# A Conformer without modulation blocks, part of its sums and copies on VectorE, ones products issued later, and a convolution lag of two

## The chip, the cores and the metric

The kernel runs on one core of a Trainium2 chip. The time is the device time of one execution in microseconds (us). A core has five engines that run side by side, each through its own queue in the order in which instructions were put there: TensorE (PE, matmuls; its weight loads are PEld), VectorE (DVE), ScalarE (ACT), GpSimd (POOL) and SyncE (SP, which here issues nearly all DMAs). They wait for each other through semaphores.

## The reference

A decoder trunk on one sequence of 1024 positions with 1024 channels. Layer 0 is an mLSTM block and layer 1 a Conformer convolution; after each comes a gated feed-forward block with a short convolution (ConvFFN). Each of the four blocks is preceded by a norm whose shift and scale, and followed by a gate, that come from a conditioning vector `c`: a product of `c` with a matrix gives 6 x 1024 numbers per layer. The block around which most of the change lies:

```python
def conformer_conv_block(h, w_pw1, b_pw1, dw_w, dw_b, ln_g, ln_b, w_pw2, b_pw2):
    a, gte = jnp.split(h @ w_pw1 + b_pw1, 2, axis=-1)
    u = a * jax.nn.sigmoid(gte)
    u = causal_dwconv(u, dw_w, dw_b)          # 31 taps
    u = jax.nn.silu(layernorm(u, ln_g, ln_b)) # over the 1024 channels
    return u @ w_pw2 + b_pw2
```

## The kernel before

**Layout.** Channels lie on the 128 partitions, in 8 blocks; the sequence lies along the free axis, in two halves `h` of 512 columns. Every float32 operand of a large product is split into two fp32r parts (`split`: ScalarE casts the high part, line 191, VectorE subtracts it, line 192), and each product of 128x128 by 128x512 becomes three matmuls (`proj_k`, line 220; `chain_products`, line 507, in products that use a scheme with seven instead of eight products). Weights come as 512 KB loads `raw` through SyncE's queue and are split into `wu`.

**What sets the order.** The program is emitted in Python order, generators interleave parts by hand (`yield` and `steps`), and a tile scheduler with priorities then gives each engine's order; tiles come from pools with a fixed number of buffers, and a tile's next user waits for the last reader.

**Modulation blocks.** `ada_product` (line 153) makes 128 channels of the modulation: a 512 KB load (line 155) and one VectorE product of 128x1024 with an accumulated sum (line 156, with a read of the accumulator); `ada_bias` (162) adds the bias and `scale_of` (186) turns scales and norm gains into `sclA`. `adas(n)` takes the next n of the list `blocks_left`: 32 of layer 0 and 48 of layer 1, in this order. They are spread over: the mLSTM's up-projection, one for each i from 3 on (13), and its z stage, 7 or 6 for each j (40); the up-projection of layer 0's ConvFFN, one in each j from 4 on until 16 (`LATER`) are left (11, there in tiles called `rb`); and the second pointwise product of the Conformer, two for each of 8 m (16, in tiles `ada`, with `c` loaded once more as `crep1`).

**The Conformer.** First the pointwise product for blocks 0 to 3 and both halves, whose 31-tap convolution runs on VectorE (`conv_dve`, 30 steps of line 1725 per block, woven in by `filler`). Blocks j = 4 to 7 (`TAIL`) follow for each half: two products (`proj`), `glu` and `spread`, and a convolution on TensorE, `conv_pe`: `spread` lays the channels out anew in `u4` (through DRAM, lines 1681 and 1683; for j = 7 by 16 ScalarE copies, line 1673), 36 matmuls with banded weights follow (line 1703; the profile shows two for each), whose bands `bands(j)` loads through POOL's queue into 4 buffers, and 16 evacuations on ScalarE add the bias (line 1712). `conv_pe(j, h)` waits in the list `ready` and runs after the two products of the next j.

**LayerNorm.** `layer_norm(h)` sums the 8 channel blocks by 8 products with a matrix of ones (line 1621, two matmuls each in the profile), centres them (1623, VectorE), squares them (1628, ScalarE), sums these by 8 more (1629), takes the inverse root (1632, 1633), and makes the operands `s8` of the next product (1637, 1638, `split`). `first` (h = 0) is stepped along the second half's loop. `second` (h = 1) begins after the last convolution and is stepped behind the second pointwise products m = 3 to 7 of h = 0; three of these products (`lead`) were started before. Each product is followed by `residual` (502, VectorE), and `following`, which squares and sums for the next norm (271, 272); L281 is that norm's product with ones. The bias of the residual is added at line 1792.

Of the kernel before, what the change touches and what calls it, by code (L numbers as in the profile page):

```python
# [15 lines left out]
P = 128  # L16
# [63 lines left out]
def trunk(ctx, tc, a):  # L80
# [20 lines left out]
    def ps(shape=(P, HS)):  # L101
        return psum.tile(list(shape), F32, tag="ps", name=nm("ps"), padded_shape=[P, HS])
# [590 lines left out]
    LATER = 16  # L693
# [17 lines left out]
    def ffn_up(layer, normed, p_d, hx, ux, es_u, other, ops):  # L711
# [149 lines left out]
        for j in range(LEAD, FB):  # L861
            s = Seven(pairs.pop(j), right, HALF)
            s.ready = set()
            if j < FB - 1:
                if layer == 0 and j > LEAD and len(blocks_left[1]) > LATER:
                    adas(1)
                    if len(blocks_left[1]) == LATER:
                        scale_of(1, 0, 0, KB)
# [129 lines left out]
    def mlstm(normed, x0, keep, k1, es1, es_x0, xp, con):  # L998
# [6 lines left out]
        if True:  # L1005
# [64 lines left out]
            with ExitStack() as es_z:  # L1070
# [65 lines left out]
                for i, h, o in stream:  # L1136
# [3 lines left out]
                    if h == NHALF - 1:  # L1140
# [10 lines left out]
                        if i >= 3:  # L1151
                            adas(1)
# [182 lines left out]
                for j in range(2, KB):  # L1335
                    s = seven[j] = Seven(pairs[j], right, HALF)
                    s.ready = set()
                    for n, q in enumerate(ORDER):
                        step(j, q)
                        adas(n < 7 - (j > 5))  # L1340
# [256 lines left out]
    def conformer(normed, following):  # L1597
# [18 lines left out]
        def layer_norm(h):  # L1616
# [3 lines left out]
            for j in range(KB):  # L1620
                pe.matmul(om, ones, at[j], start=j == 0, stop=j == KB - 1)
# [3 lines left out]
            ov = ps()  # L1625
            for j in range(KB):
                t = t512()
                sc.activation(t, at[j], AF.Square)
                pe.matmul(ov, ones, t, start=j == 0, stop=j == KB - 1)
# [31 lines left out]
        def spread(j, h, o, sg):  # L1661
# [6 lines left out]
            if j == KB - 1:  # L1668
                v.scalar_tensor_tensor(sg, o, pv("bpw1", j), sg, ALU.add, ALU.mult)
                s4 = sg.rearrange("p (n r) -> p r n", r=4)  # L1670
                for g in range(4):
                    for r in range(4):
                        sc.copy(u4[32 * r : 32 * r + 32, g, :], s4[32 * g : 32 * g + 32, r, :])
# [23 lines left out]
        def conv_pe(j, h):  # L1697
            for g in range(4):
# [12 lines left out]
                for q in range(4):  # L1711
                    sc.activation(  # L1712
                        y4[32 * g : 32 * g + 32, 3 - q, n0 : n0 + N4],
                        o[32 * q : 32 * q + 32],
                        AF.Identity,
                        bias=dwb4[32 * q : 32 * q + 32, 4 * j + g : 4 * j + g + 1],
                    )
# [33 lines left out]
        for h in range(NHALF):  # L1751
            for j in range(TAIL, KB):
# [6 lines left out]
                while ready:  # L1759
                    ready.pop(0)()  # L1760
                bands(j)
# [20 lines left out]
        ca = es_y.enter_context(phase("ca", side="right"))  # L1782
        crep = ca.tile([P, D], F32, name="crep1")
        dma(crep, crep_d)
        ada_[:] = crep, ada_tiles(ca, 2)
# [7 lines left out]
        for h in range(NHALF):  # L1793
            for m in range(KB):
# [4 lines left out]
                if not h:  # L1799
                    if m >= lead:  # L1800
                        steps(second, (1, 1, 2, 3, 3)[m - lead])
                    adas(2)
                    if m == KB - 1:
                        scale_of(1, 1, 0, KB)
# [142 lines left out]
```

## Time and profile before

| what | value |
|---|---|
| time, median of 3 runs | 2617.64 us (2614.78 to 2620.78) |
| the profiled execution | 2619.32 us, span 2617.5 us |
| mean granted TensorE clock | 0.985 |
| busy: PE, DVE, ACT, POOL | 96%, 84%, 51%, 7% |
| DMA, mean over the span | 150 GB/s |

The lines of the profile name an engine, the line of the kernel, what is written and what is read, the shape and the count. Busy times are microseconds, means are nanoseconds. Behind a bar, or in brackets, stands how long the engine was idle just before, and what it then waited for. "Clock" is the share of TensorE's full rate that was granted. The Conformer's gates (L1687) run from 1558 to 1788 us and its second pointwise product ends at 1934 us; the up-projection of layer 0's ConvFFN begins at about 890 us.

### The profile page before, as it was taken

The page shows a single profiled execution, that of the slowest core. Times are in us where ns is not written, and L with a number is a line of the kernel's source. Part 1 is how long each engine was busy: PE and PEld are TensorE (multiplying, and loading weights), DVE is VectorE, ACT ScalarE, POOL GpSimd, SP SyncE. Part 2 cuts the span into 40 slices and gives each one's busy share as a digit, 9 for nine tenths or more (in the row PEclk, how much of TensorE's full clock was granted, in tenths as well). Part 3 has the DMA queues.
Part 4 walks back from the last instruction along what each step waited for, and adds up shares of the span by engine and source line. Part 5 has one row for each costly group of instructions (what it writes and reads, how often), then busy time and mean ns, then how long its engine had stood idle before and what let it go on. Part 6 is the DMA issues. An engine that isn't in the chain of part 4 may idle for free.

```text
span 2617.5 us, 31554 instructions
## 1 busy us (share of the span) xinstructions
PE 2501.1 (96%) x11421; PEld 2044.4 (78%) x11421; DVE 2203.5 (84%) x3064; ACT 1329.6 (51%) x2005; POOL 177.4 (7%) x320
## 2 busy tenths in 40 slices
PE   6999899999999999999999999999798999999998
PEld 4788688788778778888877888877576888887787
DVE  8988986787867899998889679992889998888866
ACT  6544445776634554444544342458564444444434
POOL 0232201332100000000000000000000000000000
PEclk9999899999999999999999999999999999999999
DMA  8676355432676234433354331545823332336422
GB/s 306 191 216 206 120 201 185 132 114 70 217 271 215 93 133 161 153 117 101 116 199 148 121 140 50 171 148 165 264 85 117 121 117 101 109 97 219 151 81 97
DMA packets 149085, 393.85 MB, mean 150 GB/s; under 512 B 14848, under 2 KB 36544, under 8 KB 148928
## 3 DMA queue, kind: packets, MB, share of 16 engines
q1 hardware_dynamic: 144320, 372.95, 43.0%
q0 software_dynamic: 4608, 18.88, 2.2%
q8 instruction: 90, 1.47, 0.2%
q14 instruction: 67, 0.55, 0.1%
HBM read 299.46 MB, written 92.31 MB: 150 GB/s over the span
## 4 chain that ended last, share of the span: by engine, by line
PE 67%; DVE 18%; DMA 6%; ACT 6%; issue 3%; SPq 0%; DVEq 0%; ACTq 0%
PE ps L507 41%; PE ps L220 19%; DVE cy L1725 5%; DVE h L192 3%; PE ps L1448 2%; PE ps L1485 2%; DVE wu L192 2%; DMA ada<-in_ada 1%; ACT cy L1712 1%; DMA raw<-xc_d 1%; ACT h L191 1%; PE ps L1102 1%; DMA raw<-p_d 1%; DVE ada L156 1%; ACT wu L191 1%
## 5 line engine op out<-in xcount | busy, mean ns | idle before, releaser
L507 PE MATMUL ps<-h,wu 128*128 128x512 f32 x4704 | 1098.5, 392 | 20.5 <-DVE wu L192 6.8
L507 PEld LDWEIGHTS ps<-h,wu 128*128 128x128 f32 x4704 | 884.1, 189 | 219.9 <-DVE wu L192 10.2
L220 PE MATMUL ps<-h,wu 128*128 128x512 f32 (+1 forms) x2574 | 608.3, 392 | 13.2 <-ACT h L191 6.2
L220 PEld LDWEIGHTS ps<-h,wu 128*128 128x128 f32 x2574 | 480.3, 190 | 122.6 <-ACT h L191 7.8
L191 ACT CAST wu<-raw 128x1024 fp32r<-128x1024 f32 (+1 forms) x286 | 298.4, 1045 | 299.6 <-PE ps L220 89.5
L192 DVE TENSOR_TENSOR wu<-raw,wu 128x1024 fp32r<-128x1024 f32 (+1 forms) x286 | 346.8, 1213 | 69.6 <-ACT wu L191 68.8
L840 DVE SCALAR_TENSOR_TENSOR c<-u,par,c 128x1024 f32<-128x1024 f32 x176 | 219.9, 1279 | 2.5 <-ACT c L838 2.4
L838 ACT ACTIVATE c<-u,par 128x1024 f32<-128x1024 f32 x88 | 108.5, 1243 | 107.5 <-DVE u L627 98.2
L507 PE MATMUL ps<-h,w 128*128 128x512 f32 x648 | 157.3, 390 | 1.9 <-DVE w L192 1.9
L1725 DVE SCALAR_TENSOR_TENSOR cy<-cu,par,cy 128x512 f32<-128x512 f32 (+1 forms) x180 | 156.0, 926 | 1.1 <-ACT cy L1721 0.3
L507 PEld LDWEIGHTS ps<-h,w 128*128 128x128 f32 x648 | 121.5, 188 | 28.0 <-DVE w L192 2.8
L502 DVE SCALAR_TENSOR_TENSOR x<-ps,mod,x 128x512 f32<-128x512 f32 (+1 forms) x140 | 97.9, 715 | 43.3 <-PE ps L220 35.5
L192 DVE TENSOR_TENSOR h<-raw,h 128x512 fp32r<-128x512 f32 (+1 forms) x160 | 105.1, 688 | 25.1 <-ACT h L191 24.9
L191 ACT CAST h<-raw 128x512 fp32r<-128x512 f32 (+1 forms) x160 | 91.4, 605 | 64.7 <-DMA raw<-p_d 28.1
L1448 PE MATMUL ps<-q,h 128*128 128x512 f32 (+2 forms) x576 | 115.3, 349 | 0.3 <-DVE q L192 0.3
L1448 PEld LDWEIGHTS ps<-q,h 128*128 128x128 f32 x576 | 94.9, 189 | 16.0 <-ACT t L1513 2.0
L156 DVE SCALAR_TENSOR_TENSOR ada<-ada,crep 128x1024 f32<-128x1024 f32 x69 | 83.0, 1215 | 22.4 <-DMA ada<-in_ada 22.1
L750 ACT ACTIVATE c<-c 128x1024 f32<-128x1024 f32 x44 | 46.7, 1061 | 94.6 <-DVE c L840 94.5
L728 POOL MEMSET u<- 128x2 f32 x88 | 8.4, 99 | 1123.4 <-DVE c L840 686.6
L220 PE MATMUL ps<-h,h 128*128 128x512 f32 (+1 forms) x450 | 83.6, 347 | 0.0
L220 PEld LDWEIGHTS ps<-h,h 128*128 128x128 f32 x450 | 72.4, 189 | 10.5
L1703 PEld LDWEIGHTS ps<-u,wband 128*128 128x128 f32 x576 | 66.9, 195 | 4.1 <-issue 3.7
(282 smaller groups left out, 3240.0 us busy)
## 6 DMA issues: line engine op xcount, KB each, us to landing
raw<-in_fup SPq DMA_DIRECT2D x94, 512.0 KB, 3.6
ada<-in_ada SPq DMA_DIRECT2D x85, 512.0 KB, 4.6
p_d<-c SPq DMA_DIRECT2D x44, 512.0 KB, 2.7
raw<-in_pw SPq DMA_DIRECT2D x40, 512.0 KB, 3.8
wband<-in_w POOLq DMA_DIRECT2D x32, 576.0 KB, 5.5
raw<-in_mup SPq DMA_DIRECT2D x32, 512.0 KB, 4.4
raw<-in_fdownS SPq DMA_DIRECT2D x32, 512.0 KB, 4.2
raw<-in_mdown SPq DMA_DIRECT2D x24, 512.0 KB, 4.4
```

What stands on the lines that cost most here:

```text
L156: v.scalar_tensor_tensor(w, w, 1.0, crep, ALU.mult, ALU.mult, accum_out=mod[:, layer, b : b + 1])
L191: sc.copy(out_hi, raw)
L192: (engine or v).tensor_tensor(out_lo, raw, out_hi.bitcast(F32), ALU.subtract)
L220: pe.matmul(o, t[:, i, c : c + P], acts[k][:, j, :], start=k == 0 and n == 0, stop=k == nk - 1 and n == 2,)
L502: v.scalar_tensor_tensor(xs, o, gate, xs, ALU.mult, ALU.add)
L507: pe.matmul(o, w[:, i, k * P : (k + 1) * P], acts[k][:, j, :], start=first and k == 0 and q == 0, stop=last and k == n - 1 and q == 2, ski ...
L838: sc.activation(c, body(b), AF.Identity, scale=taps[FK - 1], bias=pv("fcb", layer, b))
L840: v.scalar_tensor_tensor(c, u[b][:, i : i + S], taps[i], c, ALU.mult, ALU.add)
L1448: pe.matmul(so[:, tlo:], xr[cc][I // nJ][:, i, I % nJ * P : (I % nJ + 1) * P], un["qs"][cc][:, j, tlo:], start=n == 0, stop=n == 3 * CB - 1,)
L1485: pe.matmul(un["num"][cc][:, tlo:], vr[I][:, i, cc * P : (cc + 1) * P], pt[:, j, tlo:], start=I == 0 and n == 0, stop=I == nJ * (hf + 1) - ...
L1703: pe.matmul(o, wd[:, 4 * d : 4 * d + 4, :].rearrange("p d c -> p (d c)"), phases[j][:, g, n0 + d : n0 + d + N4], start=d == 0, stop=d == 8,)
L1725: v.scalar_tensor_tensor(y, u[:, t + c0 : t + c1], pv("dww", t, j), y, ALU.mult, ALU.add)
```

## The change

Four things change.

1. Modulation blocks: none in the Conformer any more. The mLSTM's up-projection takes one from i = 1 on (15) and its z stage 7 for every j (42); layer 0's ConvFFN takes one for each j from 3 on, and two from j = 16 on (23). Both `scale_of` of layer 1 stand there, at the end.
2. `layer_norm(1)` adds its 8 channel blocks on VectorE (7 additions) and takes one product with ones, for the mean and for the squares; the products are issued a `yield` later, and `steps` behind m = 3 to 7 are 2, 0, 2, 4, 4 instead of 1, 1, 2, 3, 3.
3. For h = 1, half of the convolution's evacuations (odd g) and half of the copies of j = 7 (even g) go to VectorE.
4. In h = 0 a convolution runs after the products of the j after the next. The first half thus leaves two in `ready`; both run at j = 4 of the second half, with the loads of the bands of j = 7 between them.

```diff
-                if layer == 0 and j > LEAD and len(blocks_left[1]) > LATER:
-                    adas(1)
-                    if len(blocks_left[1]) == LATER:
-                        scale_of(1, 0, 0, KB)
+                adas(1 + (j >= 2 * CHUNK))
+                if layer == 0 and not blocks_left[1]:
+                    scale_of(1, 0, 0, KB)
+                    scale_of(1, 1, 0, KB)
...
-                        if i >= 3:
+                        if i:
                             adas(1)
...
-                        adas(n < 7 - (j > 5))
+                        adas(1)
...
             om = ps()
-            for j in range(KB):
-                pe.matmul(om, ones, at[j], start=j == 0, stop=j == KB - 1)
+            if h:
+                total = t512()
+                v.tensor_tensor(total, at[0], at[1], ALU.add)
+                for j in range(2, KB):
+                    v.tensor_tensor(total, total, at[j], ALU.add)
+                yield
+                pe.matmul(om, ones, total, start=True, stop=True)
+            else:
+                for j in range(KB):
+                    pe.matmul(om, ones, at[j], start=j == 0, stop=j == KB - 1)
...
             ov = ps()
+            total = t512()
             for j in range(KB):
-                t = t512()
+                t = t512() if j or not h else total
                 sc.activation(t, at[j], AF.Square)
-                pe.matmul(ov, ones, t, start=j == 0, stop=j == KB - 1)
+                if not h:
+                    pe.matmul(ov, ones, t, start=j == 0, stop=j == KB - 1)
+                elif j:
+                    v.tensor_tensor(total, total, t, ALU.add)
+            if h:
+                yield
+                pe.matmul(ov, ones, total, start=True, stop=True)
             yield
...
-                        sc.copy(u4[32 * r : 32 * r + 32, g, :], s4[32 * g : 32 * g + 32, r, :])
+                        (sc.copy if g % 2 or not h else v.tensor_copy)(
+                            u4[32 * r : 32 * r + 32, g, :], s4[32 * g : 32 * g + 32, r, :]
+                        )
...
+                    if h and g % 2:
+                        v.tensor_scalar(y, o[32 * q : 32 * q + 32], bias, None, ALU.add)
+                    else:
+                        sc.activation(y, o[32 * q : 32 * q + 32], AF.Identity, bias=bias)
...
-                while ready:
+                while len(ready) > 1 - h:
                     ready.pop(0)()
-                bands(j)
+                    if h and j == TAIL and ready:
+                        bands(KB - 1)
+                if h or j > TAIL:
+                    bands(j - 1 + h)
...
-        ca = es_y.enter_context(phase("ca", side="right"))
-        crep = ca.tile([P, D], F32, name="crep1")
-        dma(crep, crep_d)
-        ada_[:] = crep, ada_tiles(ca, 2)
...
-                if not h:
-                    if m >= lead:
-                        steps(second, (1, 1, 2, 3, 3)[m - lead])
-                    adas(2)
-                    if m == KB - 1:
-                        scale_of(1, 1, 0, KB)
+                if not h and m >= lead:
+                    steps(second, (2, 0, 2, 4, 4)[m - lead])
```

In the new kernel some lines carry other numbers: the convolution's matmuls are L1719, its evacuations L1731 (VectorE) and L1733 (ScalarE), the taps on VectorE L1741, the ones products of h = 1 L1625 and L1643, centring L1630, the squares' additions L1640, the reciprocal L1647.

TensorE before, where the first convolution (j = 4, h = 0) stands; the row above and the rows below it are products of pointwise blocks (each row three matmuls into `ps_1928`, `ps_1943`):

```order
L220 MATMUL ps_1928_13177<-h_1836_12332,wu_1924_13137 128x512 x3
L220 MATMUL ps_1928_13177<-h_1838_12337,wu_1924_13137 128x512 x3
L1703 MATMUL ps_1929_13202<-u4_1920_13119,wband_1915_13109 128x128 x9
L1703 MATMUL ps_1930_13216<-u4_1920_13119,wband_1916_13111 128x128 x9
L1703 MATMUL ps_1931_13230<-u4_1920_13119,wband_1917_13113 128x128 x9
L1703 MATMUL ps_1932_13244<-u4_1920_13119,wband_1918_13115 128x128 x9
L220 MATMUL ps_1943_13289<-h_1818_12233,wu_1927_13174 128x512 x3
```

TensorE now, where the third and the fourth convolution (j = 6 and 7, h = 0) stand at the start of the second half:

```order
L220 MATMUL ps_1988_13615<-h_1888_12622,wu_1984_13582 128x512 x3
L1719 MATMUL ps_1989_13640<-u4_1964_13412,wband_1977_13550 128x128 x9
L1719 MATMUL ps_1990_13654<-u4_1964_13412,wband_1978_13552 128x128 x9
L1719 MATMUL ps_1991_13668<-u4_1964_13412,wband_1979_13554 128x128 x9
L1719 MATMUL ps_1992_13682<-u4_1964_13412,wband_1980_13556 128x128 x9
L1719 MATMUL ps_1997_13704<-u4_1982_13560,wband_1993_13696 128x128 x9
L1719 MATMUL ps_1998_13718<-u4_1982_13560,wband_1994_13698 128x128 x9
L1719 MATMUL ps_1999_13732<-u4_1982_13560,wband_1995_13700 128x128 x9
L1719 MATMUL ps_2000_13746<-u4_1982_13560,wband_1996_13702 128x128 x9
L220 MATMUL ps_2010_13783<-h_1872_12540,wu_1987_13612 128x512 x3
```

Every convolution of the first half has moved behind one more pair of pointwise products, and the last two stand together.

VectorE before, in the second LayerNorm, from its centring on (`csc1` is the inverse root, `ada` a modulation block's tile, `x` the residual stream):

```order
L1623 SCALAR_TENSOR_TENSOR cy7_12591<-ps_2081_14443,cy7_12591 128x512
L502 SCALAR_TENSOR_TENSOR x_2079_14428<-ps_2071_14268,mod_77,x_2079_14428 128x512
...
L156 SCALAR_TENSOR_TENSOR ada_2083_14470,mod_77<-ada_2083_14470,crep1_14433 128x1024
L192 TENSOR_TENSOR wu_2111_14603<-raw_2110_14601,wu_2111_14603 128x1024
L156 SCALAR_TENSOR_TENSOR ada_2084_14473,mod_77<-ada_2084_14473,crep1_14433 128x1024
L162 TENSOR_TENSOR mod_77<-mod_77,par_72 128x2
L1633 RECIPROCAL csc1_12594<-csc1_12594 128x512
L156 SCALAR_TENSOR_TENSOR ada_2085_14478,mod_77<-ada_2085_14478,crep1_14433 128x1024
L156 SCALAR_TENSOR_TENSOR ada_2086_14481,mod_77<-ada_2086_14481,crep1_14433 128x1024
```

VectorE now, from the last convolution's evacuations to the reciprocal (`t512_2099` is the sum of the channels, `t512_2107` that of the squares):

```order
L1731 TENSOR_SCALAR cy7_12651<-ps_2094_14471,dwb4_12659 32x128 x4
L1623 TENSOR_TENSOR t512_2099_14500<-t512_2099_14500,cy7_12651 128x512
L502 SCALAR_TENSOR_TENSOR x_2096_14489<-ps_2088_14329,mod_77,x_2096_14489 128x512
L1630 SCALAR_TENSOR_TENSOR cy0_12644<-ps_2098_14499,cy0_12644 128x512
...
L1640 TENSOR_TENSOR t512_2107_14566<-t512_2107_14566,t512_2108_14568 128x512
L192 TENSOR_TENSOR wu_2119_14622<-raw_2118_14620,wu_2119_14622 128x1024
L1640 TENSOR_TENSOR t512_2107_14566<-t512_2107_14566,t512_2109_14571 128x512
L502 SCALAR_TENSOR_TENSOR x_2096_14489<-ps_2117_14594,mod_77,x_2096_14489 128x512
...
L1640 TENSOR_TENSOR t512_2107_14566<-t512_2107_14566,t512_2114_14586 128x512
L1647 RECIPROCAL csc1_12654<-csc1_12654 128x512
```

The blocks' rows are gone, the additions have come, and the reciprocal stands behind the last addition of squares. On TensorE the mean's single product stands behind the products of m = 3, the squares' behind those of m = 4 and 5.

VectorE now, late in layer 0's ConvFFN up-projection, where before no block stands (`rb` is a block's tile):

```order
L156 SCALAR_TENSOR_TENSOR rb_1494_10046,mod_77<-rb_1494_10046,ra_1227_7843 128x1024
L162 TENSOR_TENSOR mod_77<-mod_77,par_72 128x2
L753 TENSOR_TENSOR c_1423_9469<-c_1423_9469,c_1422_9452 128x1024
L192 TENSOR_TENSOR wu_1434_9549<-raw_1433_9547,wu_1434_9549 128x1024
L653 TENSOR_TENSOR t512_1424_9476<-c_1423_9469 128x512
L558 TENSOR_TENSOR t512_1436_9566<-raw_1435_9552 128x512
L156 SCALAR_TENSOR_TENSOR rb_1510_10182,mod_77<-rb_1510_10182,ra_1227_7843 128x1024
L568 TENSOR_TENSOR raw_1435_9552<-raw_1433_9547,raw_1435_9552 128x512
L192 TENSOR_TENSOR w1_1437_9571<-t512_1436_9566,w1_1437_9571 128x512
```

Between two of these blocks stand five rows, between the closest pairs elsewhere five to seven.

More of the change, by code (lines that the diff above doesn't have):

```diff
@@ L692, in trunk @@
     HALF = KB // 2
-    LATER = 16
     CHUNK = 8
@@ L1711, in conv_pe @@
                 for q in range(4):
[L1712 to L1717, printed above, removed]
+                    y = y4[32 * g : 32 * g + 32, 3 - q, n0 : n0 + N4]
+                    bias = dwb4[32 * q : 32 * q + 32, 4 * j + g : 4 * j + g + 1]
+                    if h and g % 2:
+                        v.tensor_scalar(y, o[32 * q : 32 * q + 32], bias, None, ALU.add)
+                    else:
+                        sc.activation(y, o[32 * q : 32 * q + 32], AF.Identity, bias=bias)
         def conv_dve(j, c0, c1):
```

## The prediction

> **What bounds the kernel now.** I read the page first, then windows of ten microseconds where TensorE (PE) loses time, then the chain, the groups and the timeline there.
>
> ```profile
> PE 2501.1 (96%) x11421; PEld 2044.4 (78%) x11421; DVE 2203.5 (84%) x3064; ACT 1329.6 (51%) x2005; POOL 177.4 (7%) x320
> ...
> PE 67%; DVE 18%; DMA 6%; ACT 6%; issue 3%; SPq 0%; DVEq 0%; ACTq 0%
> ```
>
> TensorE issues matmuls nearly all the time, so only gaps on TensorE, matmuls at a lower clock, and removed matmuls can give time back. A third of the chain is other work, so the gaps must be found. Columns below: window; its length; busy us of PE, PEld, DVE, ACT, POOL (with instructions); granted clock; DMA share; GB/s.
>
> ```profile
> 1100.00:1150.00 50.00, 50.00 (x222) 41.40 (x221) 47.10 (x56) 25.14 (x30) 0.60 (x6) 1.00 0.37 128
> 1150.00:1200.00 50.00, 50.00 (x223) 41.39 (x222) 45.22 (x53) 22.74 (x26) 0.49 (x5) 1.00 0.30 101
> 1200.00:1250.00 50.00, 50.00 (x222) 41.31 (x221) 43.10 (x52) 21.75 (x26) 0.49 (x5) 1.00 0.29 97
> ...
> 1650.00:1660.00 10.00, 7.17 (x47) 6.70 (x46) 10.00 (x12) 4.01 (x7) 0.71 (x2) 0.83 0.33 103
> ...
> 1800.00:1810.00 10.00, 6.23 (x22) 4.48 (x21) 2.48 (x4) 9.86 (x19) 0.00 (x0) 0.85 0.03 12
> ...
> 1880.00:1890.00 10.00, 5.26 (x20) 3.09 (x18) 8.16 (x14) 7.19 (x11) 0.00 (x0) 1.00 0.73 221
> 1890.00:1900.00 10.00, 1.33 (x3) 0.82 (x3) 8.30 (x14) 1.89 (x3) 0.13 (x2) 0.62 0.52 170
> ```
>
> At full rate a 128x512 matmul takes 50/222 = 0.225 us. In the conformer the rate breaks at 1650, near 1752, at 1805 and, worst, from 1860 to 1900: there the second pointwise product runs beside the second LayerNorm and 16 modulation blocks. The chain names what it waits for:
>
> ```profile
> 1851.97 5.04 DMA ada<-in_ada
> ...
> 1858.30 5.03 DMA ada<-in_ada
> ...
> 1884.39 4.51 DMA ada<-in_ada
> ...
> 1898.67 2.08 PE ps L281 x2
> ```
>
> The last links are block loads and VectorE (DVE) work, until TensorE resumes at 1898.67 with the sums of the next norm (L281). The groups of 1825 to 1900:
>
> ```profile
> 1825.00:1900.00 75.00, 58.22 (x208) 39.92 (x206) 57.22 (x90) 39.94 (x55) 0.13 (x2) 0.90 0.77 256
> ...
> L156 DVE SCALAR_TENSOR_TENSOR ada<-ada,crep 128x1024 f32<-128x1024 f32 x16 | 19.5, 1218 | 6.4 <-DMA ada<-in_ada 6.3
> L192 DVE TENSOR_TENSOR wu<-raw,wu 128x1024 fp32r<-128x1024 f32 x7 | 8.5, 1219 | 2.3 <-ACT wu L191 2.3
> ...
> L1623 DVE SCALAR_TENSOR_TENSOR cy<-ps,cy 128x512 f32<-128x512 f32 x8 | 4.9, 680 | 11.7 <-PE ps L1621 11.7
> L272 DVE TENSOR_TENSOR acc<-acc,t 128x512 f32<-128x512 f32 x7 | 4.8, 686 | 0.3
> L156 DVE DVE_READ_ACCUMULATOR ada<-ada,crep 128x1 f32 x16 | 1.3, 82 | 0.0
> ...
> L1792 ACT ACTIVATE x<-x,gb 128x1024 f32<-128x1024 f32 x8 | 9.1, 1139 | 3.8 <-DMA x<-x_d 3.7
> L1628 ACT ACTIVATE t<-cy 128x512 f32<-128x512 f32 x8 | 4.8, 615 | 0.0
> ...
> L220 PE MATMUL ps<-h,wu 128*128 128x512 f32 x169 | 46.3, 428 | 5.7 <-DVE h L192 3.2 <-ACT h L191 2.4
> L1629 PE MATMUL ps<-t,ones 128*128 128x512 f32 x16 | 7.4, 592 | 0.0
> L1621 PE MATMUL ps<-cy,ones 128*128 128x512 f32 x16 | 7.0, 592 | 0.0
> L281 PE MATMUL ps<-acc,ones 128*128 128x512 f32 x2 | 2.1, 1142 | 11.1 <-DVE acc L272 11.1
> ```
>
> The smaller losses, and what a new kind of operation may cost:
>
> ```profile
> 1653.76 9.78 PE L1703 MATMUL ps<-u,wband 128*128 128x128 f32 x72 [2.83 <-DMA u<-u_d]
> ...
> 1712.45 8.20 PE L1703 MATMUL ps<-u,wband 128*128 128x128 f32 x72
> ...
> 1714.92 0.53 POOL L1658 DMA_DIRECT2D wband<-in_w  x1 [12.37 <-PE ps L1703]
> ...
> 1752.09 5.40 PE L1629 MATMUL ps<-t,ones 128*128 128x512 f32 x8 [2.17 <-ACT t L1628]
> ...
> 1804.15 0.75 DVE L1637 SCALAR_TENSOR_TENSOR t<-cy,par,csc 128x512 f32<-128x512 f32 x1 [12.57 <-ACT u L1673]
> ...
> 1807.32 10.11 PE L220 MATMUL ps<-h,wu 128*128 128x512 f32 x36 [3.77 <-ACT h L191]
> ...
> 1825.31 7.03 PE L1621 MATMUL ps<-cy,ones 128*128 128x512 f32 x16
> ```
> ```profile
> L1712 ACT ACTIVATE cy<-ps,dwb 32x128 f32<-32x128 f32 x128 | 62.2, 486 | 8.5 <-PE ps L1703 6.8
> L1239 DVE COPY ipre<-ps 32x128 f32<-32x128 f32 x1 | 0.3, 271 | 0.0
> ```
>
> **The change, part by part.**
>
> *A, lag of two.* The first convolution on TensorE waited 2.83 us for its input's way through DRAM and then ran 9.78 us instead of 8.20. One more block pair (48 matmuls, 10.8 us) now lies ahead of it: both go, 2.83 + 1.58 = 4.4. What is late next: two convolutions stand back to back at the start of the second half, and the later one's bands load into buffers that the earlier one frees. A first band load was issued 2.47 us after a convolution's start (1714.92 against 1712.45); the page gives
>
> ```profile
> wband<-in_w POOLq DMA_DIRECT2D x32, 576.0 KB, 5.5
> ```
>
> so it lands at 2.5 + 5.5 = 8.0, against 8.2 for the first convolution: cost between 0 and 6 (landings twice as long), I take 1, near the median.
>
> *B, h=0 variance.* The wait of 2.17 us, and 5.40 for 8 matmuls that take 3.5 at L1621's rate (7.03/16 = 0.44 each): 4.1. Squares stood behind evacuations on ScalarE (ACT), half of which leave it (8 x 0.486 = 3.9): gone.
>
> *C, first pointwise products.* Wait 3.77, and 10.11 for 36 matmuls worth 8.1: 5.8. ScalarE was the late one, with DVE idle for 12.57 us; it sheds 16 evacuations (7.8 us) and 8 copies. On DVE an operation of that shape costs between 0.27 (the copy from PSUM, the nearest row) and 0.49 (ScalarE's row); 24 of them take 6.5 to 11.7 us, which that idle time hides. If it did not, the excess would come straight back off C, and the 8 of the last convolution stand ahead of the tail.
>
> A rule that speaks against this: by the Trainium skill, "VectorE: DVE Perf Modes", section "Two Vector instructions with no wait between them", an instruction whose input or output begins in another group of 32 partitions than the one before it starts only when everything earlier has finished. These evacuations change that group each time, so by that rule they would stand at the dear end, and the sum would be about 2 less for the 8 in the tail. No row of this trace has such a series.
>
> By the Trainium skill, "TensorE: Matmul & The Clock Gate", Part 1, the clock halves only after about 3.4 us of idleness. The trace speaks against that as a threshold: 0.83 was granted in 1650 to 1660 after a wait of 2.83. By that rule the slower matmuls in A and B would have another cause and would stay, and the sum would be 3.5 less.
>
> *D, the tail.* From the last convolution's end (1825.3) to L281 (1898.7) are 73.4 us. There now remain 168 products (37.8 us) and, instead of 32 ones matmuls, 4 (1.8 us): 39.6 if nothing waits. DVE had 57.2 us; 16 blocks leave (20.8 with their reads) and 14 adds come (14 x 0.686 = 9.6): 46.0. So DVE has more than TensorE here. It can no longer idle 11.7 us at the start: the seven mean adds are work that precedes the single product, six of them before the last convolution has ended. What binds next is the single variance product. TensorE reaches it after 72 products (16.2) and the mean's product (0.9), 17.1 us after the convolution's end. DVE can start its centrings at +6.5, when 24 products and the mean's product are done, and the new order then gives it 8 centrings, 7 adds, 5 residuals and 3 weight subtractions before the last add is out: 20 x 0.69 + 3 x 1.22 = 17.5, so +24. ScalarE's own line (9.1 of residual biases, 4.8 of squares, some casts) is shorter. The wait is 7, a new one, where the eight separate products of before let squares come one by one. After it matmuls run slower for a while, as after the waits in A and B (1.6 and 1.9): 1.6. And L281 still waits for the last squares and sums behind DVE's 46.0 us; 11.1 was with 20.8 us more of DVE work, I take 3. So 39.6 + 7 + 1.6 + 3 = 51: gain 22.4. Bounds: 39.6 (no wait at all, gain 33.8) and 62 (DVE's 46.0 plus the idle start of 11.7 and 4 of smaller waits, as now, gain 11.4).
>
> *E, 12 more blocks in layer 0's FFN up-projection.* 12 x 1.30 = 15.6 us of DVE, with biases and scales about 16.9. By their place among the steps 14 blocks now stand where 11 stood, up to 1092, and 9 more behind them, up to about 1200. The cover there is DVE's idle time of 1100 to 1200, 2.9 + 4.8 = 7.7; the other 9.2 have to be carried as a backlog into 1200 to 1250, where 6.9 are idle. Just before, with blocks already there, DVE is full and TensorE loses nothing:
>
> ```profile
> 1050.00:1100.00 50.00, 50.00 (x222) 41.35 (x221) 49.65 (x67) 23.59 (x28) 0.59 (x6) 1.00 0.45 156
> ...
> L156 DVE SCALAR_TENSOR_TENSOR rb<-rb,ra 128x1024 f32<-128x1024 f32 x11 | 13.4, 1217 | 0.2 <-DMA rb<-in_ada 0.2
> ...
> L156 DVE SCALAR_TENSOR_TENSOR rb<-rb,ra x11: 1211/1218/1226, 955.3 to 1091.7; 128x1024 f32<-128x1024 f32 x11
> ```
>
> Cost 0 to 16.9; of the 9.2 that are not covered at their place I take 4, since a full DVE left PE at 50.00 there and so has some room to run late. If the cover is gone, TensorE waits for weight subtractions, one for one. The mLSTM's 4 more blocks (5.2 us of DVE) go into a stage that has 53: 0 to 5, taken as 0 by the same row. All these loads go through SyncE's queue, where the weights' loads (raw) stand behind them; a load that must wait for its buffer holds those up too (rival 3).
>
> Sum: 4.4 + 4.1 + 5.8 + 22.4 - 1 - 4 = 31.7. The profiled execution took 2619.32 (span 2617.5), 1.7 above the median of 2617.64, so **2619.3 - 31.7 - 1.7 = 2586** as a median (2585.9).
>
> **Rivals.**
>
> 1. *The tail turns DVE-bound.* DVE's 46.0 us against TensorE's 39.6 speak for it; that adds, unlike blocks, wait for no load speaks against. D gives 11.4: 2586 + 11 = **2597**.
> 2. *The up-projection pays.* DVE is full, nothing hides: 13 more, 2586 + 13 = **2599**. For: 49.65 of 50 above. Against: 50.00 of PE beside it, and idle DVE after 1100.
> 3. *Slower: the single block buffer.* In the up-projection each block is loaded into one buffer that a temporary tile also uses. A load is issued only when the buffer is free; if DVE reaches the next block sooner than it lands, DVE sits it out, and with it the weight subtractions and soon TensorE. The page's landing of block loads is 4.6:
>
> ```profile
> ada<-in_ada SPq DMA_DIRECT2D x85, 512.0 KB, 4.6
> ```
>
>    if 2 of that are uncovered, 23 blocks cost 46: 2586 + 46 = **2632**. The gain is gone from 31.7 / 23 = 1.4 us a block on, that is where less than 4.6 - 1.4 = 3.2 us of DVE work lie between two blocks. The closest pairs of the new order have five to seven rows between them, 4 to 6 us. Against it too: 0.2 us of waiting in eleven blocks.
> 4. *The waits of A to C reappear.* DVE's convolution taps (its 10.00 of 10 at 1650) or ScalarE hold those places anyway, and the shorter queues change nothing: only D counts, 14.3 less: **2600**. Against: DVE's idle 12.57 and the ScalarE releaser at 1807.
>
> **Numbers.** Chances: forecast 0.54, rival 1 0.15, rival 2 0.13, rival 4 0.09, several of these at once so that nothing is left 0.03, rival 3 0.06. Forecast and rivals 1, 2, 4 are faster: 0.91; same 0.03; slower 0.06. About 0.2%, 5.2 us, is what a measurement can tell from no change. The range reaches down to 2569 (no wait in the tail, no costs: 2586 - 11.4 - 5 = 2569.6) and up to 2604 (rival 2's full 16.9, 2599, and the bands' further 5).
>
> **What would show it.** Right: no wait ahead of the first convolution, no wait above 1 us at the h=0 variance and at the first pointwise products; from the last convolution to L281 about 51 us with one wait of some 7 before the single variance product; PE 50 of 50 from 1100 to 1250 with DVE near 49. Wrong: a block load as releaser of DVE in the up-projection (rival 3), PE below 49 there (rival 2), a tail of 60 us (rival 1), or the old releasers in the conformer (rival 4).

## The result, and the profile after

The changed kernel takes 2586.41 us in the median of 4 runs (2583.13 to 2590.53), the kernel before 2617.51 us in 4 runs: ratio 0.9885 with a 95% interval of 0.9866 to 0.9904, so faster by 31 us, with an interval from 25 to 35. A second series on another chip gave 0.9881 (0.9868 to 0.9895). The profiled execution of the changed kernel has a span of 2588.8 us and is the slowest of its four runs (2590.53 us).

The page after, against the row shown of before: TensorE is busy 14 us less, VectorE 23 us more; the granted clock is 0.985 as before.

```profile
PE 2487.0 (96%) x11393; PEld 2038.6 (79%) x11393; DVE 2226.8 (86%) x3121; ACT 1311.4 (51%) x1965; POOL 177.5 (7%) x320
```

The windows of the up-projection, where the blocks went, and of the place of the first convolution:

```profile
1050.00:1100.00 50.00, 49.98 (x220) 40.84 (x219) 49.56 (x66) 24.38 (x29) 0.59 (x6) 1.00 0.47 148
1100.00:1150.00 50.00, 50.00 (x222) 41.40 (x221) 49.81 (x67) 22.89 (x26) 0.50 (x5) 1.00 0.53 173
1150.00:1200.00 50.00, 50.00 (x222) 41.24 (x221) 49.50 (x67) 23.15 (x28) 0.50 (x5) 1.00 0.48 164
1200.00:1250.00 50.00, 50.00 (x222) 41.23 (x221) 47.55 (x58) 25.08 (x30) 0.60 (x6) 1.00 0.39 132
...
1650.00:1660.00 10.00, 10.00 (x46) 8.29 (x45) 10.00 (x12) 2.11 (x3) 0.00 (x0) 1.00 0.38 105
```

VectorE has filled up from 1100 to 1200 (49.81 and 49.50, before 47.10 and 45.22), and TensorE still issues 222 matmuls in each 50 us. The clock at 1650 is 1.00 instead of 0.83. TensorE's timeline through the Conformer (start, length, matmuls, and in brackets the wait ahead):

```profile
1660.52 5.29 PE L1719 MATMUL ps<-u,wband 128*128 128x128 f32 x46
1666.00 5.28 PE L220 MATMUL ps<-h,wu 128*128 128x512 f32 x22 [0.18 <-DVE wu L192]
1671.12 3.06 PE L1719 MATMUL ps<-u,wband 128*128 128x128 f32 x26
...
1703.89 14.36 PE L1719 MATMUL ps<-u,wband 128*128 128x128 f32 x126
1718.70 2.25 PE L1719 MATMUL ps<-u,wband 128*128 128x128 f32 x18 [0.46 <-DMA wband<-in_w]
...
1746.64 7.03 PE L1638 MATMUL ps<-t,ones 128*128 128x512 f32 x16
...
1791.29 16.58 PE L220 MATMUL ps<-h,wu 128*128 128x512 f32 x72
1807.71 8.20 PE L1719 MATMUL ps<-u,wband 128*128 128x128 f32 x72
1815.67 5.70 PE L220 MATMUL ps<-h,wu 128*128 128x512 f32 x24
1821.20 1.02 PE L1625 MATMUL ps<-t,ones 128*128 128x512 f32 x2
1821.66 11.48 PE L220 MATMUL ps<-h,wu 128*128 128x512 f32 x48
1840.74 2.05 PE L1643 MATMUL ps<-t,ones 128*128 128x512 f32 x2 [7.60 <-DVE t L1640]
1841.80 23.84 PE L220 MATMUL ps<-h,wu 128*128 128x512 f32 x96
1870.78 2.08 PE L281 MATMUL ps<-acc,ones 128*128 128x512 f32 x2 [5.14 <-DVE acc L272]
```

The first convolution no longer waits (two pieces, 46 and 26 matmuls, 8.35 us). The h=0 variance is one run of 16 matmuls, the first pointwise products one run of 72, without a wait. In the tail two waits stand where before there were many: 7.60 us ahead of the single product of the squares and 5.14 ahead of the next norm.

The stages, cut at the starts of L281's matmuls and at the end of the last convolution (1825.31 before, 1815.67 after), in the two profiled executions:

| stage | before | after | difference | predicted |
|---|---|---|---|---|
| start to L281 of the first ConvFFN (mLSTM) | 840.2 | 842.2 | +2.0 | 0 |
| to L281 ahead of the Conformer (ConvFFN, layer 0) | 703.0 | 704.9 | +1.9 | +4 |
| to the last convolution's end | 282.1 | 268.6 | -13.5 | -13.3 |
| tail, to L281 of the last ConvFFN | 73.4 | 55.1 | -18.3 | -22.4 |
| the rest | 718.8 | 718.0 | -0.8 | 0 |
| span | 2617.5 | 2588.8 | -28.7 | -31.7 |

A second profile of the changed kernel reached the first of these marks at 838.1, 4 us earlier, with the same program: one profile is good to no better than some 4 us in the first stage, and its +2.0 means nothing. In that second profile the other stages are 703.8, 269.2, 55.4 and 718.3 us.

### The profile page after: what moved, and what is told of

Its sections match the earlier page's. It is cut to its first block, busy times and chain, and to the rows that moved or that the text cites. A ratio compares the mean times of both kernels' runs of the same rounds, so it can differ in the third digit from the quotient of the medians.

```text
span 2588.8 us, 31511 instructions
## 1 busy us (share of the span) xinstructions
PE 2487.0 (96%) x11393; PEld 2038.6 (79%) x11393; DVE 2226.8 (86%) x3121; ACT 1311.4 (51%) x1965; POOL 177.5 (7%) x320
## 4 chain that ended last, share of the span: by engine, by line
PE 67%; DVE 12%; issue 11%; DMA 6%; ACT 4%; SPq 0%; POOL 0%; DVEq 0%; ACTq 0%; POOLq 0%
PE ps L507 41%; PE ps L220 17%; DVE h L192 3%; PE ps L1447 2%; PE ps L1484 2%; PE ps L1719 1%; DVE wu L192 1%; DMA raw<-in_mup 1%; ACT h L191 1%; PE ps L1101 1%; DMA raw<-xc_d 1%; DMA raw<-p_d 1%; DMA raw<-in_mdown 1%; DVE xc L1144 1%; DVE x L786 1%
## 5 line engine op out<-in xcount | busy, mean ns | idle before, releaser
L1741 DVE SCALAR_TENSOR_TENSOR cy<-cu,par,cy 128x512 f32<-128x512 f32 (+1 forms) x180 | 156.0, 928 | 1.0 <-ACT cy L1737 0.3
L1447 PEld LDWEIGHTS ps<-q,h 128*128 128x128 f32 x576 | 94.9, 189 | 16.1 <-ACT t L1512 2.0
L156 DVE SCALAR_TENSOR_TENSOR ada<-ada,crep 128x1024 f32<-128x1024 f32 x57 | 68.5, 1216 | 14.8 <-DMA ada<-in_ada 14.8
L220 PE MATMUL ps<-go,wu 128*128 128x512 f32 x288 | 67.0, 391 | 0.0
```

Of the source, the lines that this page charges most:

```text
L156: v.scalar_tensor_tensor(w, w, 1.0, crep, ALU.mult, ALU.mult, accum_out=mod[:, layer, b : b + 1])
L220: pe.matmul(o, t[:, i, c : c + P], acts[k][:, j, :], start=k == 0 and n == 0, stop=k == nk - 1 and n == 2,)
L1447: pe.matmul(so[:, tlo:], xr[cc][I // nJ][:, i, I % nJ * P : (I % nJ + 1) * P], un["qs"][cc][:, j, tlo:], start=n == 0, stop=n == 3 * CB - 1,)
L1741: v.scalar_tensor_tensor(y, u[:, t + c0 : t + c1], pv("dww", t, j), y, ALU.mult, ALU.add)
```

## The experiments

Theory: blocks, lag and queues are separate gains; in the tail VectorE and the blocks' loads were the bound, so moving the blocks gives most of it. Rivals: the 28 ones matmuls are the tail's gain; the blocks are paid for where they went; the lag or the new VectorE operations give nothing by themselves. Times are medians, and ratios are against the kernel before, run on the same chip.

**The changed kernel again.**

> The changed kernel once more, as the measure for the others. Every theory: about 2586 us, 31 below before.

2584.55 us, ratio 0.9881 (0.9868 to 0.9895).

**Only the blocks moved.**

```diff
-                if not h:
-                    if m >= lead:
-                        steps(second, (1, 1, 2, 3, 3)[m - lead])
-                    adas(2)
...
+                if not h and m >= lead:
+                    steps(second, (1, 1, 2, 3, 3)[m - lead])
```

> Only part 1: the modulation blocks leave the Conformer, all else as before. Theory (the tail was held by VectorE and its loads): VectorE falls from 57.2 to 36 us there, TensorE has 37.8 + 14 = 52 us, with some 6 of waits the tail takes 58 instead of 73.4, and the blocks cost nothing at their new place: 2602. Rival (the gain of the tail is the 28 ones matmuls, 12 us): 2612 or more. Rival (the blocks cost their full 17 us in the up-projection): 2617 or more, with PE below 50 of 50 between 1100 and 1250 us.

2592.07 us, ratio 0.9912 (0.9898 to 0.9925): 22.5 us of the 30 come from this part alone, more than expected. The tail is 53.0 us, not 58. In the window of the tail TensorE has hardly a gap, with all 32 ones matmuls:

```profile
1821.90:1875.00 53.10, 52.48 (x203) 37.47 (x203) 36.31 (x47) 37.82 (x54) 0.13 (x2) 1.00 0.51 183
```

**All but the blocks.** The blocks stay in the Conformer, with the tables and the tile of before; sums, copies, evacuations and lag as in the changed kernel.

> Parts 2 to 4 without part 1: the blocks stay in the Conformer as before. Theory: the lag and the shorter ScalarE queue give their 13.5 us, the tail gets nothing or loses, since VectorE has 57.2 + 9.6 = 67 us there and waits for loads: tail 73 to 80, time 2604 to 2611. Rival (the ones matmuls make the gain): 12 us more gain, 2592.

2601.90 us, ratio 0.9953 (0.9937 to 0.9969): 12.6 us faster than before, near the theory's 13.5 for lag and queues alone (the rival had 12 more). The tail takes 71.7 us, 1.7 less than before (first row before, second row this run):

```profile
1825.30:1898.70 73.40, 56.62 (x203) 38.84 (x201) 57.22 (x90) 39.64 (x55) 0.13 (x2) 0.91 0.78 259
1815.80:1887.50 71.70, 48.25 (x175) 35.38 (x174) 63.63 (x102) 37.51 (x51) 0.14 (x2) 0.81 0.79 271
```

TensorE has 28 matmuls less and is busy 8.4 us less, at a clock of 0.81; VectorE is busy 63.63 of 71.70 us. With blocks on VectorE's queue the removed matmuls are worth next to nothing.

**All but the sums.** `layer_norm(1)` and its steps as before, everything else changed:

```diff
-            if h:
-                total = t512()
-                v.tensor_tensor(total, at[0], at[1], ALU.add)
...
-                if not h and m >= lead:
-                    steps(second, (2, 0, 2, 4, 4)[m - lead])
+                if not h and m >= lead:
+                    steps(second, (1, 1, 2, 3, 3)[m - lead])
```

> The changed kernel with the LayerNorm of h = 1 as before (16 products with ones on TensorE, steps 1, 1, 2, 3, 3). Theory: the tail is 52 us of TensorE and about 5 of waits, 57, against 55.1 measured: 2588, so the additions on VectorE give only about 2 because their 12 us on TensorE come back as the wait of 7.6 and of 5.1. Rival: the 28 matmuls are worth their 12 us, 2598.

2578.56 us, ratio 0.9859 (0.9844 to 0.9875): 6.0 us *faster* than the changed kernel run beside it. Both theories missed the sign: the additions on VectorE cost time. The two intervals still overlap a little; the trace, and the two kernels further down that also leave out the additions of squares, point the same way. The tail is 52.7 us (first fence), and TensorE's rows in it show why:

```profile
1809.70:1862.50 52.80, 52.48 (x203) 37.54 (x202) 38.18 (x51) 35.93 (x50) 0.14 (x2) 1.00 0.51 183
```
```profile
1822.11 4.45 PE L1628 MATMUL ps<-t,ones 128*128 128x512 f32 x10
1826.88 1.12 PE L1628 MATMUL ps<-t,ones 128*128 128x512 f32 x2 [0.32 <-ACT t L1627]
1827.44 1.03 PE L220 MATMUL ps<-h,wu 128*128 128x512 f32 x2
...
1862.51 1.02 PE L281 MATMUL ps<-acc,ones 128*128 128x512 f32 x2
1862.97 33.25 PE L220 MATMUL ps<-h,wu 128*128 128x512 f32 x144
```

With eight products the squares are summed as they come, between other matmuls, and no wait exceeds 0.32 us; L281 is not waited for at all, and the 144 matmuls behind it take 33.25 us instead of 34.82. In the changed kernel the 28 matmuls (28 x 0.44 = 12.3 us) are gone, and waits of 7.60 and 5.14 (12.7 us) have come. The additions and the later issue of the products went together here, so this run does not tell them apart; the kernel with the mean alone on VectorE (below) issues the mean's product late too.

**The lag of before.**

```diff
-                while len(ready) > 1 - h:
+                while ready:
                     ready.pop(0)()
-                    if h and j == TAIL and ready:
-                        bands(KB - 1)
-                if h or j > TAIL:
-                    bands(j - 1 + h)
+                bands(j)
```

> The changed kernel with the convolution lag of before (one pair of products). Theory (A): the first convolution waits 2.8 us for its input again and runs 1.6 slower, the back-to-back pair with its 0.5 to 1 us of wait for bands goes: 2585 + 3.5 = 2588.5. Rival (the wait is hidden by something that binds anyway): 2585.

2590.22 us, ratio 0.9906 (0.9893 to 0.9919), some 6 us slower than the changed kernel (0.9881 and 0.9885), more than the 3.5 expected. The intervals overlap, but the trace has the size: the stage up to the last convolution's end takes 273.5 us, against 268.6 and 269.2 in the changed kernel's two profiles, 4.3 to 4.9 more. The wait is back, and the slower matmuls were dearer than in the kernel before (72 took 11.17 us, there 9.78, and 8.20 at full rate):

```profile
1652.30 11.17 PE L1719 MATMUL ps<-u,wband 128*128 128x128 f32 x72 [3.08 <-DMA u<-u_d]
```

Wait and slower matmuls are 6.0 us here, less the 0.5 to 0.9 of the bands' wait in the changed kernel's two profiles.

**All evacuations and copies on ScalarE.**

```diff
-                        (sc.copy if g % 2 or not h else v.tensor_copy)(
+                        sc.copy(
...
-                    if h and g % 2:
+                    if False:
```

> The changed kernel with all evacuations and copies on ScalarE. Theory (B and C, ScalarE's queue is late): the waits of 2.2 before the h=0 variance and 3.8 before the first pointwise products come back with their slower matmuls, 9.9 in all: 2595. Rival (ScalarE was late for VectorE's sake, or one more pair of products from the lag covers the waits): 2585 to 2587, VectorE's new operations of 0.44 us each give nothing.

2592.90 us, ratio 0.9909 (0.9894 to 0.9925): some 6 to 8 us slower than the changed kernel (6 to 7 by the ratios, 8 by the medians), 10 expected. Both waits return, with ScalarE as releaser (second and third row), that at the variance only by half:

```profile
1716.52 2.25 PE L1719 MATMUL ps<-u,wband 128*128 128x128 f32 x18 [2.92 <-DMA wband<-in_w]
...
1749.07 3.70 PE L1638 MATMUL ps<-t,ones 128*128 128x512 f32 x8 [1.02 <-ACT t L1636]
...
1802.59 0.50 PE L220 MATMUL ps<-h,wu 128*128 128x512 f32 x1 [3.77 <-ACT h L191]
```

The first row is probably chance, since the kernels are alike there: the bands' wait between the two convolutions was 0.46 and 0.94 us in the changed kernel's profiles, 1.10 and 1.69 in two experiments, and in all others with the lag of two between 0.7 and 1.4. A second profile of this kernel, which could show it, is not there.

**The mean on VectorE, the squares on TensorE.**

```diff
-            total = t512()
             for j in range(KB):
-                t = t512() if j or not h else total
+                t = t512()
                 sc.activation(t, at[j], AF.Square)
-                if not h:
-                    pe.matmul(ov, ones, t, start=j == 0, stop=j == KB - 1)
-                elif j:
-                    v.tensor_tensor(total, total, t, ALU.add)
-            if h:
-                yield
-                pe.matmul(ov, ones, total, start=True, stop=True)
+                pe.matmul(ov, ones, t, start=j == 0, stop=j == KB - 1)
...
-                    steps(second, (2, 0, 2, 4, 4)[m - lead])
+                    steps(second, (1, 1, 2, 4, 4)[m - lead])
```

> The changed kernel with the mean's sum on VectorE (one product with ones) and the squares' sum by 8 products on TensorE as they come, steps 1, 1, 2, 4, 4. Theory (the additions of squares are what the wait of 7.6 and the later one of 5.1 hang on; those of the mean lie in VectorE's idle time): TensorE has 45.8 us in the tail, a wait of a few us before the squares and none at the next norm, tail about 50 against 55 now and 53 with 16 products: 2576. Rival (the issue of the products later than before is what costs, whoever adds): the wait stays, tail 55 or more, 2585.

2578.09 us, ratio 0.9860 (0.9846 to 0.9873). The tail is 50.0 us, as expected, and the wait of 7.6 is gone. The waits lie elsewhere than expected: at most 0.43 us at a time between the products of the squares, where a few were expected ahead of them, and 1.97 at L281, where none was:

```profile
1829.18 1.13 PE L1636 MATMUL ps<-t,ones 128*128 128x512 f32 x2 [0.43 <-ACT t L1635]
...
1863.90 1.35 PE L281 MATMUL ps<-acc,ones 128*128 128x512 f32 x2 [1.97 <-DVE acc L272]
1864.47 34.86 PE L220 MATMUL ps<-h,wu 128*128 128x512 f32 x144
```

The time is the same as with all 16 products, though the tail is 2.7 shorter: it ends in a wait again, and the matmuls behind are slower again (34.86).

**35 blocks in the up-projection.**

```diff
-                        if i:
+                        if i >= 13:
                             adas(1)
...
-                adas(1 + (j >= 2 * CHUNK))
+                adas(2)
```

> The changed kernel with 35 instead of 23 blocks in layer 0's up-projection (two for each j from 3 on; the mLSTM takes 45). VectorE gets 15.6 us more there; what it had idle with 23 blocks is 0.7 from 1100 to 1200, 2.5 to 1250 and 6.9 to 1300. Theory (the cover is VectorE's idle time, with some backlog): 15.6 - 10.1 = 5 us are not covered, and with the part that lies before 1100 it becomes 5 to 10: 2590 to 2595. Rival (the single buffer, 4.6 us of landing between close blocks): 2600 or more with VectorE waiting for loads. Rival (TensorE is never held by VectorE there): 2585.

2584.99 us, ratio 0.9888 (0.9875 to 0.9901): no difference to 23 blocks. The theory's 5 to 10 us are not there, nor is a wait of VectorE for loads that would count (first fence: us, times). But this time is a net one: the same 12 blocks left the mLSTM. In the trace the up-projection's stage takes 705.8 us, 1 to 2 more than with 23 blocks (704.9 and 703.8), and the first stage 834.5 instead of 842.2 and 838.1; by its spread that is not a sure gain, and whether the one hides the other stays open. The windows:

```profile
  DMA rb<-in_ada: 1.2, 3
```
```profile
1000.00:1050.00 50.00, 48.05 (x210) 39.44 (x211) 49.84 (x65) 24.80 (x30) 0.51 (x6) 1.00 0.48 160
...
1200.00:1250.00 50.00, 50.00 (x222) 41.42 (x221) 49.90 (x65) 23.23 (x26) 0.60 (x6) 1.00 0.45 150
1250.00:1300.00 50.00, 50.00 (x222) 41.22 (x221) 48.68 (x64) 28.58 (x38) 0.30 (x3) 1.00 0.46 153
```

From 1000 to 1300 us VectorE is busy 49.6 us or more of each 50, in the last window 48.68; TensorE loses 2 us, once. The blocks simply run on, to 1268 us.

**ScalarE's biases later.**

```diff
-        for k in range(KB):
-            sc.activation(x[:, k, :], x[:, k, :], AF.Identity, bias=gb2[:, k : k + 1])
...
+                if not h:
+                    sc.activation(x[:, m, :], x[:, m, :], AF.Identity, bias=gb2[:, m : m + 1])
                 residual(o, mod[:, L, 16 + m : 17 + m], m, h * HS)
```

> The changed kernel with ScalarE's bias of the residual (8 operations of 1.14 us, all ahead of the squares) issued one by one ahead of the residual that needs it. Theory (the wait of 7.6 before the squares' product is VectorE's queue of about 20 operations): ScalarE's shorter queue changes it by at most 1: 2585. Rival (ScalarE's queue, where the last square starts at 1838 behind these biases): the wait falls by up to 4 us, 2581.

2586.08 us, ratio 0.9891 (0.9875 to 0.9908), wait 7.52. This tells nothing of the rival: the scheduler put the biases between the squares much as before, and the last square starts 16.2 us behind the start of the mean's product in both.

**The same behind the mixed kernel.** Residuals and biases of h=0 are emitted behind the LayerNorm's steps:

```diff
+                if not h and m >= lead:
+                    steps(second, (1, 1, 2, 4, 4)[m - lead])
+                waiting.append((o, m))
+                while waiting and (h or m >= lead):
+                    o, k = waiting.pop(0)
+                    if not h:
+                        sc.activation(x[:, k, :], x[:, k, :], AF.Identity, bias=gb2[:, k : k + 1])
+                    residual(o, mod[:, L, 16 + k : 17 + k], k, h * HS)
+                    following(h, k)
```

> The kernel with the mean on VectorE and the squares on TensorE, with biases and residuals of the first half issued behind the LayerNorm's steps. Theory: its tail of 50.0 us has 45.8 us of TensorE and ends in a wait of 2.0 before the next norm; if residuals no longer stand ahead of centring, squares come about 2 us sooner: 2575. Rival (the sums of the next norm, which follow the residuals, are now later): the wait at the next norm grows, 2578 or more.

2576.86 us (2576.70 to 2577.44), ratio 0.9854 (0.9835 to 0.9872): the fastest median, but not to be told from the two others without the squares' additions. Its tail is 49.8 us. Neither theory nor rival came as put: the squares' first product starts 11.9 us behind the convolution's end, as without this edit, and the wait at L281 fell to 1.58. The matmuls behind it take 33.25 us.

## Why the prediction was right, point by point

The forecast of 2586 met 2586.4. That close a match is luck: between the two profiled executions the sum is 28.7 us instead of 31.7. There the tail gave 4 us less than said and the up-projection cost 2 less, and the profiled execution of the changed kernel happens to lie 4.1 us above its median.

**A, B, C** were right together: 13.5 us against 13.3. The three waits named are gone, and each returns when its cause is put back, that at the variance by half. The slower matmuls went with the waits (8.35, 7.03 and 16.58 us for the matmuls of the three places), so the prediction's other reading, that those of A and B would stay, is not borne out. The lag was undervalued (4 to 6 us, by stage and by time, instead of 3.4 net), since the price of the slower matmuls behind the wait varies: 1.6 us in the profile of before, 3.0 in the experiment. The ScalarE share was overvalued (6 to 8 instead of 9.9), because the wait at the variance is halved without it: 1.02 instead of 2.17. The lag is the part that differs there, since with the lag of before and all evacuations on ScalarE (only the blocks moved) the wait is 2.11.

**Bands**, taken as 1: 0.46 and 0.94 in the changed kernel, up to 2.92 in an experiment.

**New VectorE operations** were bounded by 0.27 and 0.49 us; the rows after lie near the upper and at the lower bound:

```profile
L1731 DVE TENSOR_SCALAR cy<-ps,dwb 32x128 f32<-32x128 f32 x32 | 14.2, 444 | 3.5 <-PE ps L1719 3.0
...
L1687 DVE COPY u<-t 32x128 f32<-32x128 f32 x8 | 2.1, 266 | 0.1
```

The rule of the Trainium skill weighed there ("VectorE: DVE Perf Modes", section "Two Vector instructions with no wait between them") fits the evacuations, 444 ns against 271 for a lone copy of that shape from PSUM; the copies, which change group as well, show 266, so these rows do not settle it. No time hung on it, not the 2 us weighed either: in the tail the last evacuations and the sum behind them end at 1818.6, ahead of the mean's product at 1821.2.

**D** was right in its mechanism and 4 us too large. The wait before the single product was named, put at 7 and measured at 7.60; the wait at L281 was put at 3 and measured at 5.14, and TensorE was busy 42.4 us, 2.8 over the 39.6 of full rate where 1.6 was put; most of that are the 96 matmuls behind the first wait, 23.84 us or 2.2 over full rate. So of the 4 us, 0.6 lie in the first wait, 2.1 in that at L281 and 1.2 in slower matmuls. The window of the tail:

```profile
1815.70:1870.80 55.10, 42.37 (x175) 32.82 (x174) 44.32 (x61) 37.54 (x52) 0.13 (x2) 0.92 0.51 179
```

That the first wait came out so near is luck in part. VectorE's start of the centrings was put at +6.5. It was +8.8, as the timeline of VectorE and ScalarE shows:

```profile
1817.87 0.69 DVE L1623 TENSOR_TENSOR t<-t,cy 128x512 f32<-128x512 f32 x1
1822.63 1.15 ACT L1807 ACTIVATE x<-x,gb 128x1024 f32<-128x1024 f32 x1 [6.72 <-DMA x<-x_d]
1823.82 0.75 DVE L502 SCALAR_TENSOR_TENSOR x<-ps,mod,x 128x512 f32<-128x512 f32 x1 [5.26 <-ACT x L1807]
1824.48 1.28 DVE L1630 SCALAR_TENSOR_TENSOR cy<-ps,cy 128x512 f32<-128x512 f32 x2
```

A residual stands ahead of the centring in VectorE's queue; it waits for ScalarE's bias, and that for the residual stream's reload. VectorE sat idle for 5.26 us there, the last 1.6 of them with the mean's product done (1822.2). Its 23 operations up to the last addition then took 16.1 us instead of the 17.5 reckoned, so the two errors nearly cancel: the addition ended at +24.9, forecast +24.

The larger error is the 3 us put at L281, which was a guess from a wait of 11.1 and not worked out. In the trace VectorE goes from 1854 to 1870.7 without a wait, with the next product's weight subtractions between the last sums, while TensorE is done at 1865.6.

More important is what D didn't ask: whether the ones matmuls were worth removing. In the working they are the 28 matmuls, some 12 us, by which TensorE's work falls to 39.6 us; as much came back as waits. The experiments show that the blocks alone give the tail of 53.0, and that with them gone TensorE was the bound, without a gap. The additions then removed work from the engine that was the bound, but put a chain (centring, squares, 7 additions, one product) in front of an in-order queue: products that could have filled the wait stand behind the single one. What the tail then takes is the length of that chain. It is the chain of the squares: with the mean alone summed on VectorE the tail is shorter than with all 16 products, 50.0 against 52.7 us. Not tried was the single product of squares issued later still, behind the other two products of the first half, which could have filled the wait.

Behind the tail the waits cost once more. The 144 matmuls behind L281 take 34.82 us after the wait of 5.14 and 33.25 without a wait, and the granted clock in the first 10 us of them is 0.83 against 1.00. That 1.6 lies behind the mark at which the tail was measured, and explains a part of why 2.4 us of tail are 6.0 us of time. The Trainium skill's page "TensorE: Matmul & The Clock Gate", Part 1, has idleness followed by a stretch at half rate, and these rows agree. Its 3.4 us as a threshold is not borne out: the wait of 1.97 has 34.86 behind it (clock 0.83), that of 1.58 33.25 (clock 1.00).

**E** was over-sized: 4 taken, 1 to 2 in the two profiles, 3 with 35 blocks in the profile and nothing in the time. The row that said so was in the prediction (49.65 of VectorE beside 50.00 of TensorE); the working then charged the uncovered part all the same. VectorE must run ahead of TensorE there, since it is full for 150 us and more while TensorE loses nothing; how far ahead was not measured.

**Rivals.** Rival 1 (tail bound by VectorE, 62 us): half true. Both waits are for VectorE's queue, but VectorE is busy only 44.3 us and the tail takes 55.1, nearer to the forecast's 51. Rival 2 (up-projection pays): false, since TensorE is at 50.00 of 50 from 1100 to 1250 and the stage costs 1 to 2 us, not 17. Rival 3 (single buffer): false; VectorE waited 0.4 us for 23 loads and 1.2 for 35, since the loads land in 3.7 us and five rows of VectorE lie between the closest blocks:

```profile
rb<-in_ada SPq DMA_DIRECT2D x23, 512.0 KB, 3.7
```

Rival 4 (A to C reappear): false, the waits are gone.

**The parts together.** Taken one at a time, the blocks give 22 us, the lag 4 to 6 and ScalarE's share 6 to 8, and the sums cost 6: 26 to 30, where the whole gives 30.

**Open.** The kernels without the squares' additions gain 6.0 to 8 us over the changed one; tail (2.4) and slower matmuls behind it (1.6) make 4.0 with all 16 products. The rest lies behind the tail: that stage takes 715 to 718 us in the six profiles with the blocks moved and the squares added on VectorE, 712 to 715 in the four with the blocks moved and the squares on TensorE. Why, beyond the slower matmuls, stays open; some of it may lie in the next up-projection's start (below). Whether ScalarE's squares have a part in the 7.60 wait no run separates: the one meant for it did not change the order. The trace speaks for VectorE alone: it has no wait between the centrings' start at 1824.5 and the last addition's end at 1840.6, so in this order it is never held up by a square (the last one ended at 1838.1).

## What to carry to other kernels

Work that can run anywhere should leave the stage whose chain is tight for one with slack, and an engine at 99% is no sign that there is none: look whether the engine it feeds loses anything, and raise the load until it does. Before taking matmuls off TensorE, ask whether they fill waits: eight small products that take their inputs as they come cost 0.88 us each and let others pass between, while one product at the end of a chain of additions makes an in-order queue wait for the whole chain. And a part of a change that is right on its own (less ScalarE queue, one more lag) should be judged alone, since the sum can hide a part that loses.

## What the runs showed of the hardware

The price of a short wait is not fixed. The same wait of 2.59 us at the same place of the last up-projection was followed by 20 matmuls in 4.63 + 3.29 us in one profile and in 3.90 + 2.48 in another, from the changed kernel (its second profile) and from the one without the sums:

```profile
1960.27 4.63 PE L507 MATMUL ps<-h,wu 128*128 128x512 f32 x10 [2.59 <-DVE wu L192]
1964.70 3.29 PE L507 MATMUL ps<-h,w 128*128 128x512 f32 x10
```
```profile
1954.09 3.90 PE L507 MATMUL ps<-h,wu 128*128 128x512 f32 x10 [2.59 <-DVE wu L192]
1957.83 2.48 PE L507 MATMUL ps<-h,w 128*128 128x512 f32 x10
```

So 1.5 us hang on something other than the length of the wait. The h=0 variance shows the same: behind a wait of 2.17 us its last 8 matmuls took 5.40 us in the kernel before, behind 2.11 us 3.70 with only the blocks moved. What it hangs on these runs do not show; that the moment at which a wait falls decides is a guess. Runs of one kernel spread by several us as well, 2582.79 to 2595.07 in six runs of one of the experiments, whether for this reason or another.
